# Four pieces of the next first layer ahead of a unit's pairs instead of three

## The chip, the cores and the metric

The kernel runs on one core of one Trainium2 chip. The metric is device time in microseconds (us) of one execution. Before the change three timed runs gave 1337.73, 1338.77 and 1339.29 us, a median of 1338.77 us.

## The reference, cut to what matters

The program is one layer of a diffusion backbone over 1024 latent tokens of width 1024. After a mixing half (convolution, Fourier mixing, attention, state space) comes the feed-forward half, which the change concerns:

```python
hx = modulate(rmsnorm(x_mid, g_norm_mlp[l]), sh2, sc2)
x = x_mid + gt2 * squared_relu_mlp(hx, w_ff1[l], b_ff1[l], w_ff2[l], b_ff2[l])

def squared_relu_mlp(h, w1, b1, w2, b2):
    return jnp.square(jax.nn.relu(h @ w1 + b1)) @ w2 + b2
```

The hidden width is 4096, everything is fp32 on the outside, and a final RMSNorm closes the program.

## The kernel before, in words

**Splitting.** A matmul operand is split into a high part (`w2h`, `fh`, `th`: a rounded copy made by ScalarE, ACT in the profile) and a low part (`w2l`, `fl`, `tl`: the difference). Three matmuls (high by high, high by low, low by high; `mm3w`, L1472) stand for one exact product. Weights are split by ACT (L1455) and GpSimd (POOL, L1456); hidden values by ACT (L1487) and VectorE (DVE, L1488).

**Units.** The hidden width is cut into 16 units of 256. A unit has a first layer (hidden values from `h`) and a second layer (their share of the output). Tokens stand in two halves of 512. From unit 2 on, the first layer of a unit is a recursion with seven products (`a11`, `a12`, `s1` to `s4`, `a22`) in place of eight. Each product is cut into two *pieces*, h0 and h1, of six matmuls each: 14 pieces, which `q_pieces` lists in that order. The weights of `s1` to `s4` are sums that DVE makes: L1605 (`s1`, into the one tile `ws`), L1607 (`s2`, in place), L1609 (`s3`, into a `w1r` tile), L1611 (`s4`, into `ws`).

**Pairs.** The second layer of a unit is four *pairs* p0 to p3. A pair is a recursion with seven products of three matmuls, in the order a0, a1, b1, b0, c0, c1, and d; the d of a pair is issued inside the next one, after its a1. They use PSUM banks: a0 in `fa`, a1 in `fc`, b1 in `fb`; b0 adds onto what a0 left in `fa`, c0 onto `fb`, c1 and then d onto `fa`. After each product DVE adds the bank, scaled, to the output tile `X` (`add_x`, L1493). So b0 may not start until DVE has read `fa` after a0, and d not until DVE has read it after c1.

**What runs beside.** While the pairs of unit u-1 run, pieces of the first layer of unit u are put between their products, so that DVE has time for its additions. In order, before the change: three pieces ahead (`a11` h0, h1 and `a12` h0); a0 of p0; one piece; a1, b1, b0; one piece; c0, c1; then p1, p2, p3 with one piece each between b0 and c0; one piece and the last d; and the remaining five pieces as a tail.

**What follows a piece.** After the second piece of a product come its `post` steps: L1624 copies a bank to `ft`, L1627 adds a bank to it (with `a12`: bank `qc`), L1479 and L1480 are the squared ReLU on ACT, and `part` (L1487, L1488) is the split. `s3` h0 triggers the split of hidden value (0,0). `a22` h1, the last piece of a unit, triggers a longer chain, over three entries: L1636 to L1638 (`sums`, from `s4` h1), the splits of t1, (1,0), t2, t3, t4, and L1645 (`sum_21`). These are what a0, a1, b1, b0, c1 and d of the next pairs read.

**What sets the order.** `Pieces.emit(AHEAD)` writes the instructions of PE, ACT, POOL and DVE in a fixed order. Before entry i of the sequence (a piece or one product) it issues the weight split of every entry up to i + 5 that has none yet. So where an entry stands also decides where its weight split stands in the queues of DVE (for `s1` to `s4`), ACT and POOL. Each engine works its queue in order. `w2h` and `w2l` have six buffers each. The DMAs on SP's queue are ordered by a scheduler.

Of the kernel before, what the change touches and what calls it, by code (L numbers as in the profile page):

```python
# [49 lines left out]
def body(tc, A, out, dbg=None):  # L50
# [1717 lines left out]
    with tc.manual_schedule(engines=MAN):  # L1768
        for u in range(2, NU2):
            q = q_pieces(u)  # L1770
            for _ in range(4 if u == 2 else 3):
                q.pop(0)()
            (plain_pieces if u == 2 else pair_pieces)(u - 1, q)
            for f in q:
                f()
        pc.emit(AHEAD)
# [158 lines left out]
```

## Time and profile before

| what | value |
|---|---|
| median of the timed runs | 1338.77 us |
| the profiled execution's own time | 1341.13 us |
| its span | 1339.0 us |
| granted TensorE clock, mean of the span | 0.947 |
| PE busy | 1197.4 us, 89% |
| DVE busy | 1068.4 us, 80% |
| POOL busy | 808.6 us, 60% |
| ACT busy | 652.7 us, 49% |

The span is the time from the first to the last instruction of one profiled execution. The loop that the change touches lies between about 721 and 1286 us of it. One turn of the loop takes 40.49 us (its wait stands at 814.14 us in one unit and at 854.63 us in the next). A row of a timeline gives the start, the duration, engine, line, operation, output<-inputs, and in brackets the engine's idle time just before and what ended it; "x2" means two instructions merged into the row. A row of the waits gives total us, times, longest us. A row by windows gives the window, its length, the busy us of PE, weight loads, DVE, ACT and POOL with the numbers of instructions, the granted clock, the DMA share and GB/s.

### The profile page before, as it was taken

How to read it: one execution, taken by the hardware profiler on the slowest of the kernel's cores; microseconds unless marked ns; L12 is line 12 of the kernel's file. 1: busy time of each engine (PE TensorE's matmuls, PEld its weight loads, DVE VectorE, ACT ScalarE, POOL GpSimd, SP SyncE). 2: the span in 40 equal slices, each digit the busy share in tenths (PEclk: the TensorE clock that was granted, in tenths of full speed). 3: DMA queues.
4: the chain of work that ended last, by engine and by line, in shares of the span. 5: the costliest groups of instructions: out<-in, count | busy, mean ns of one | idle time of the engine just before them, and what ended most of it. 6: DMA issues, size and time to landing. Idle time of an engine off the chain costs nothing.

```text
span 1339.0 us, 18718 instructions
## 1 busy us (share of the span) xinstructions
PE 1197.4 (89%) x6188; PEld 965.5 (72%) x6188; DVE 1068.4 (80%) x1636; ACT 652.7 (49%) x1337; POOL 808.6 (60%) x1002
## 2 busy tenths in 40 slices
PE   5889878898865999899999999999999999999996
PEld 3657656777655777777778777777877777777775
DVE  4775999869999768658695579888888888888867
ACT  5254333323446565554664445555545555444555
POOL 3825677372556734015367477777877778787754
PEclk9989898998975999898999999999999999999998
DMA  9455232161153544323121121111211112211113
GB/s 344 142 164 164 81 125 79 47 199 66 51 177 94 175 128 142 109 78 143 32 77 43 40 64 32 48 56 56 63 56 32 52 52 63 64 41 39 56 40 126
DMA packets 75058, 121.77 MB, mean 91 GB/s; under 512 B 16977, under 2 KB 35154, under 8 KB 74962
## 3 DMA queue, kind: packets, MB, share of 16 engines
q1 hardware_dynamic: 62802, 113.24, 26.9%
q10 hardware_dynamic: 12160, 7.34, 1.8%
q8 instruction: 49, 0.80, 0.3%
q14 instruction: 47, 0.39, 0.1%
HBM read 106.68 MB, written 13.88 MB: 90 GB/s over the span
## 4 chain that ended last, share of the span: by engine, by line
PE 48%; DVE 29%; ACT 5%; issue 4%; POOL 4%; DMA 3%; SPq 1%; ACTq 0%; DVEq 0%; POOLq 0%
PE fa L1472 11%; PE qa L1472 6%; PE qb L1472 5%; PE fb L1472 5%; DVE cacc L1015 5%; DVE tl L1488 3%; PE fc L1472 2%; DVE fl L1488 2%; PE f L1472 2%; PE p_t L1270 2%; PE mm L1097 2%; PE mm L1472 2%; DVE Ss L698 2%; DVE Ss L697 1%; DVE X L1493 1%
## 5 line engine op out<-in xcount | busy, mean ns | idle before, releaser
L1456 POOL TENSOR_TENSOR w2l<-w2r,w2h 128x128 fp32r<-128x128 f32 (+1 forms) x232 | 177.4, 766 | 75.3 <-ACT w2h L1455 68.1
L1493 DVE SCALAR_TENSOR_TENSOR X<-fa,gt2c,X 128x512 f32<-128x512 f32 x216 | 159.4, 745 | 13.0 <-PE fa L1472 13.0
L1455 ACT ACTIVATE w2h<-w2r 128x128 fp32r<-128x128 f32 (+1 forms) x232 | 85.8, 387 | 150.8 <-POOL w2r L1706 79.8
L1456 POOL TENSOR_TENSOR w2l<-w1r,w2h 128x256 fp32r<-128x256 f32 x136 | 108.5, 814 | 57.7 <-ACT w2h L1455 34.0
L235 POOL TENSOR_TENSOR wlo<-wraw,whi 128x1024 fp32r<-128x1024 f32 x30 | 75.2, 2508 | 102.0 <-ACT whi L233 82.9
L1493 DVE SCALAR_TENSOR_TENSOR X<-fb,gt2c,X 128x512 f32<-128x512 f32 x108 | 80.5, 745 | 35.4 <-PE fb L1472 35.3
L1456 POOL TENSOR_TENSOR w2l<-ws,w2h 128x256 fp32r<-128x256 f32 x84 | 67.9, 815 | 41.4 <-ACT w2h L1455 40.1
L1015 DVE SCALAR_TENSOR_TENSOR cacc<-cv,wdw,cacc 128x512 f32<-128x512 f32 x92 | 92.3, 1047 | 0.6
L364 PE MATMUL mm<-xl,whi 128*128 128x512 f32 x192 | 81.2, 424 | 3.8 <-DVE xl L220 3.8
L364 PE MATMUL mm<-xh,whi 128*128 128x512 f32 x192 | 77.3, 423 | 7.0 <-ACT xh L218 5.8
L1472 PE MATMUL fa<-th,w2h 128*128 128x512 f32 x156 | 63.2, 405 | 19.7 <-DVE X L1493 19.7
L364 PE MATMUL mm<-xh,wlo 128*128 128x512 f32 x192 | 80.6, 420 | 0.0
L1455 ACT ACTIVATE w2h<-w1r 128x256 fp32r<-128x256 f32 x136 | 53.9, 409 | 47.5 <-DVE w1r L1609 16.5
L1472 PE MATMUL qa<-cb,w2h 128*128 128x512 f32 x224 | 70.7, 397 | 0.7 <-ACT ft L1624 0.7
L1488 DVE TENSOR_TENSOR fl<-ft,fh 128x512 fp32r<-128x512 f32 x64 | 56.9, 906 | 12.8 <-ACT fh L1487 12.7
L1472 PE MATMUL fa<-th,w2l 128*128 128x512 f32 x156 | 61.7, 396 | 0.6 <-POOL w2l L1456 0.6
L1472 PE MATMUL fa<-tl,w2h 128*128 128x512 f32 x156 | 61.5, 394 | 0.0
L1013 POOL TENSOR_TENSOR pacc<-pacc,ptmp 128x512 f32<-128x512 f32 x24 | 37.4, 1559 | 29.8 <-ACT ptmp L1012 29.8
L1455 ACT ACTIVATE w2h<-ws 128x256 fp32r<-128x256 f32 x84 | 33.1, 410 | 42.4 <-DVE ws L1605 20.4
L1472 PEld LDWEIGHTS fa<-th,w2h 128*128 128x128 f32 x156 | 29.3, 188 | 30.8 <-DVE X L1493 25.2
L364 PEld LDWEIGHTS mm<-xh,whi 128*128 128x128 f32 x192 | 38.1, 201 | 18.4 <-ACT xh L218 7.2
L1472 PEld LDWEIGHTS qa<-cb,w2h 128*128 128x128 f32 x224 | 42.0, 188 | 11.2 <-ACT ft L1624 1.1
(788 smaller groups left out, 3945.3 us busy)
## 6 DMA issues: line engine op xcount, KB each, us to landing
w2r<-in_w_ff SPq DMA_DIRECT2D x68, 256.0 KB
wmB<-in_wmodB SPq DMA_DIRECT2D x32, 512.0 KB
w1r<-in_w_ff SPq DMA_DIRECT2D x64, 256.0 KB
wm<-in_wmodA SPq DMA_DIRECT2D x16, 512.0 KB
wraw<-in_w_in SPq DMA_DIRECT2D x12, 512.0 KB
x<-in_xT SPq DMA_DIRECT2D x8, 512.0 KB
wraw<-in_w_out SPq DMA_DIRECT2D x8, 512.0 KB
kr<-k_d SPq DMA_DIRECT2D x16, 256.0 KB
```

Source lines behind the costliest of these rows:

```text
L235: (lo_eng or G).tensor_tensor(lo, raw, hi.bitcast(F32), ALU.subtract)
L364: PE.matmul(o, a_[:, k, :], b_[hf][k], start=k == 0 and i == 0, stop=k == 7 and i == 2)
L698: V.tensor_tensor_scan(Ss[b_, i, g, ::-1], r_[b_], src[b_, g, ::-1], 0.0, ALU.mult, ALU.add)
L1013: G.tensor_tensor(pacc, pacc, t, ALU.add)
L1015: V.scalar_tensor_tensor(acc, x(k), w(k), acc, ALU.mult, ALU.add)
L1097: PE.matmul(o, a_[:, 2 * kk + c, :], b_, start=c == 0 and i == 0, stop=c == 1 and i == 2)
L1270: PE.matmul(po[:, j * 64:j * 64 + 64], ptt[:, i * P:(i + 1) * P], rv, start=i == 0, stop=i == 4, skip_group_check=True)
L1455: S.activation(hi, a, AF.Copy)
L1456: G.tensor_tensor(lo, a, hi.bitcast(F32), ALU.subtract)
L1472: PE.matmul(o, a_[:, i, :], m_, start=start and j == 0, stop=stop and j == 2, skip_group_check=True)
L1488: V.tensor_tensor(lo, t, hi.bitcast(F32), ALU.subtract)
L1493: return V.scalar_tensor_tensor(x, o, gt2(k), x, ALU.mult, ALU.add).ins
```

## The change

One number: for every unit four pieces are issued ahead of the pairs. For unit 2 it was four already.

```diff
         for u in range(2, NU2):
             q = q_pieces(u)
-            for _ in range(4 if u == 2 else 3):
+            for _ in range(4):
                 q.pop(0)()
             (plain_pieces if u == 2 else pair_pieces)(u - 1, q)
             for f in q:
```

The number of instructions stays as it was. In 13 turns (units 3 to 15) each piece from `a12` h1 on moves one place to the front: `a12` h1 stands ahead of a0 of p0, `s1` h0 after a0, `s1` h1 after b0, `s2` h0 and h1 in p1 and p2, `s3` h0 between b0 and c0 of p3, `s3` h1 before the last d, and four pieces are left for the tail.

**DVE at the start of a unit's pairs.** The splits of t1, (1,0) are `fl`, those of t2, t3, t4 are `tl`; X<-fa is the addition after a0. Before:

```order
L1638 TENSOR_TENSOR ft<-ft 128x512
L1488 TENSOR_TENSOR fl<-ft,fh 128x512 x2
L1488 TENSOR_TENSOR tl<-ft,th 128x512
L1645 TENSOR_TENSOR ft<-ft 128x512
L1488 TENSOR_TENSOR tl<-ft,th 128x512 x2
L1605 TENSOR_TENSOR ws<-w1r 128x512
L1493 SCALAR_TENSOR_TENSOR X<-fa,gt2c,X 128x512
L1627 TENSOR_TENSOR ft<-ft,qc 128x512
```

And now:

```order
L1638 TENSOR_TENSOR ft<-ft 128x512
L1488 TENSOR_TENSOR fl<-ft,fh 128x512
L1605 TENSOR_TENSOR ws<-w1r 128x512
L1488 TENSOR_TENSOR fl<-ft,fh 128x512
L1488 TENSOR_TENSOR tl<-ft,th 128x512
L1645 TENSOR_TENSOR ft<-ft 128x512
L1488 TENSOR_TENSOR tl<-ft,th 128x512 x2
L1627 TENSOR_TENSOR ft<-ft,qc 128x512
L1493 SCALAR_TENSOR_TENSOR X<-fa,gt2c,X 128x512
```

L1605, the weight sum of `s1`, has moved from the end of the splits to a place between the first two, and L1627 has moved ahead of the addition after a0.

**ACT at the same place.** w2h<-ws is the weight split of `s1` (h0, then h1), `fh` and `th` are the high parts of t1, (1,0), t2, t3, t4, and L1479 and L1480 the squared ReLU that follows L1627. Before:

```order
L1487 ACTIVATE fh<-ft 128x512 x2
L1487 ACTIVATE th<-ft 128x512
L1455 ACTIVATE w2h<-w2r 128x256
L1487 ACTIVATE th<-ft 128x512
L1624 COPY ft<-qa 128x512
L1487 ACTIVATE th<-ft 128x512
L1455 ACTIVATE w2h<-ws 128x256
L1455 ACTIVATE w2h<-w2r 128x256
L1479 ACTIVATE ft<-ft,colf 128x512
L1480 ACTIVATE ft<-ft 128x512
```

And now:

```order
L1487 ACTIVATE fh<-ft 128x512
L1455 ACTIVATE w2h<-ws 128x256
L1487 ACTIVATE fh<-ft 128x512
L1487 ACTIVATE th<-ft 128x512 x2
L1624 COPY ft<-qa 128x512
L1455 ACTIVATE w2h<-w2r 128x256
L1487 ACTIVATE th<-ft 128x512
L1479 ACTIVATE ft<-ft,colf 128x512
L1480 ACTIVATE ft<-ft 128x512
L1455 ACTIVATE w2h<-ws 128x256
```

The split of `s1` h0 now stands between the high parts of t1 and (1,0), and that of `s1` h1 behind the squared ReLU.

**DVE in the last pair, p3.** The X rows are the additions after b1 and b0, after c0 and c1, and after the last d; L1611 is the weight sum of `s4`, `fl` the low part of (0,0), and L1627 the addition of bank `qa` after `s3` h1. Before:

```order
L1493 SCALAR_TENSOR_TENSOR X<-fb,gt2c,X 128x512
L1493 SCALAR_TENSOR_TENSOR X<-fa,gt2c,X 128x512
L1611 TENSOR_TENSOR ws<-w1r,ws 128x512
L1493 SCALAR_TENSOR_TENSOR X<-fb,gt2c,X 128x512
L1493 SCALAR_TENSOR_TENSOR X<-fa,gt2c,X 128x512
L1488 TENSOR_TENSOR fl<-ft,fh 128x512
L1493 SCALAR_TENSOR_TENSOR X<-fa,gt2c,X 128x512
L1627 TENSOR_TENSOR ft<-ft,qa 128x512
```

And now:

```order
L1493 SCALAR_TENSOR_TENSOR X<-fb,gt2c,X 128x512
L1493 SCALAR_TENSOR_TENSOR X<-fa,gt2c,X 128x512
L1611 TENSOR_TENSOR ws<-w1r,ws 128x512
L1488 TENSOR_TENSOR fl<-ft,fh 128x512
L1493 SCALAR_TENSOR_TENSOR X<-fb,gt2c,X 128x512
L1493 SCALAR_TENSOR_TENSOR X<-fa,gt2c,X 128x512
L1627 TENSOR_TENSOR ft<-ft,qa 128x512
L1493 SCALAR_TENSOR_TENSOR X<-fa,gt2c,X 128x512
```

The low part of (0,0) has moved ahead of the additions after c0 and c1. On ACT its high part stands directly behind the split that waits for L1611.

## Rows read from the trace of the kernel before

**Rows 1.** By windows: one turn of the loop, busy times and clock.

```profile
804.99:845.48 40.49, 38.98 (x170) 31.42 (x168) 33.81 (x47) 21.26 (x49) 31.21 (x47) 1.00 0.16 52
```

**Rows 2.** Waits of PE from 720 to 1286 us.

```profile
PE fa L1472 <- DVE X L1493: 19.7, 13, 1.5
```

**Rows 3.** Timeline of PE, start of a unit's pairs.

```profile
804.99 0.39 PE L1472 MATMUL qa<-mh,w2h 128*128 128x512 f32 x1
...
814.14 0.50 PE L1472 MATMUL fa<-th,w2h 128*128 128x512 f32 x1 [1.51 <-DVE X L1493]
...
814.95 0.63 PE L1472 MATMUL qb<-c,w2h 128*128 128x512 f32 x2
...
816.35 0.40 PE L1472 MATMUL fb<-fh,w2h 128*128 128x512 f32 x1
...
817.75 0.40 PE L1472 MATMUL fa<-fh,w2h 128*128 128x512 f32 x1
```

**Rows 4.** Timeline of DVE, start of a unit's pairs.

```profile
807.25 1.81 DVE L1488 TENSOR_TENSOR fl<-ft,fh 128x512 fp32r<-128x512 f32 x2
808.99 1.22 DVE L1488 TENSOR_TENSOR tl<-ft,th 128x512 fp32r<-128x512 f32 x1
810.13 1.22 DVE L1645 TENSOR_TENSOR ft<-ft 128x512 f32<-128x512 f32 x1
...
812.75 0.68 DVE L1605 TENSOR_TENSOR ws<-w1r 128x512 f32<-128x512 f32 x1
813.35 0.74 DVE L1493 SCALAR_TENSOR_TENSOR X<-fa,gt2c,X 128x512 f32<-128x512 f32 x1
814.01 0.67 DVE L1627 TENSOR_TENSOR ft<-ft,qc 128x512 f32<-128x512 f32 x1
```

**Rows 5.** Timeline of ACT, start of a unit's pairs.

```profile
806.45 1.14 ACT L1487 ACTIVATE fh<-ft 128x512 fp32r<-128x512 f32 x2
...
813.46 0.42 ACT L1455 ACTIVATE w2h<-ws 128x256 fp32r<-128x256 f32 x1 [1.44 <-DVE ws L1605]
813.78 0.40 ACT L1455 ACTIVATE w2h<-w2r 128x256 fp32r<-128x256 f32 x1
814.72 0.73 ACT L1479 ACTIVATE ft<-ft,colf 128x512 f32<-128x512 f32 x1 [0.54 <-DVE ft L1627]
...
816.02 0.60 ACT L1455 ACTIVATE w2h<-w2r 128x256 fp32r<-128x256 f32 x2
```

**Rows 6.** Timeline of POOL, start of a unit's pairs.

```profile
808.47 1.18 POOL L1456 TENSOR_TENSOR w2l<-w1r,w2h 128x256 fp32r<-128x256 f32 x1
809.62 1.18 POOL L1456 TENSOR_TENSOR w2l<-w2r,w2h 128x256 fp32r<-128x256 f32 x1
810.76 0.91 POOL L1708 TENSOR_TENSOR w2r<-w2r 128x128 f32<-128x128 f32 x1
813.95 0.74 POOL L1456 TENSOR_TENSOR w2l<-ws,w2h 128x256 fp32r<-128x256 f32 x1 [2.28 <-ACT w2h L1455]
```

**Rows 7.** Timeline of PE, last pair of a unit.

```profile
792.53 0.40 PE L1472 MATMUL fa<-th,w2h 128*128 128x512 f32 x1
...
795.32 0.40 PE L1472 MATMUL fa<-th,w2h 128*128 128x512 f32 x1
...
797.42 0.39 PE L1472 MATMUL fa<-th,w2h 128*128 128x512 f32 x1
```

**Rows 8.** Timeline of DVE, last pair of a unit.

```profile
794.10 0.74 DVE L1493 SCALAR_TENSOR_TENSOR X<-fa,gt2c,X 128x512 f32<-128x512 f32 x1
794.76 0.68 DVE L1611 TENSOR_TENSOR ws<-w1r,ws 128x512 f32<-128x512 f32 x1
...
796.21 0.75 DVE L1493 SCALAR_TENSOR_TENSOR X<-fa,gt2c,X 128x512 f32<-128x512 f32 x1
797.06 0.69 DVE L1488 TENSOR_TENSOR fl<-ft,fh 128x512 fp32r<-128x512 f32 x1
```

**Rows 9.** Timeline of PE after the loop.

```profile
1295.92 1.12 PE L1472 MATMUL f<-fh,c 128*128 128x512 f32 x3 [2.33 <-ACT fh L1487]
```

## The prediction

> **What bounds the kernel now.** I read the busy times by windows first, then the waits of PE, then the timelines of the four engines around those waits. In one turn of the loop PE is busy for 38.98 of 40.49 us at a granted clock of 1.00, with DVE next at 33.81 us [rows 1]. So PE bounds the loop, and what it does not use is a single wait: 13 times about 1.5 us, 19.7 us in all, for an addition of DVE to X [rows 2]. The 1.51 us by which PE's 38.98 fall short of the turn's 40.49 are that one wait. So the most that any reordering can win here is 19.7 us, and every new gap of PE is paid in full, since nothing later in the turn gives time back.
>
> The place of the wait is b0 of the first pair. PE starts `a11` h0 of the next unit at 804.99; b0 should follow 33 matmuls later and starts at 814.14, after 1.51 us of idling [rows 3]. It waits for the addition after a0, which runs from 813.35 to 814.09 because DVE works through a packed chain of splits from 807.25 on, the weight sum L1605 last [rows 4]. The spacing of PE's matmuls without a wait is 1.40 us for six (814.95 to 816.35) [rows 3].
>
> **The change part by part.** No instruction is added or removed, so busy sums stay; only waits can move. I work in the clock of this turn and take everything up to the first `fl` at 807.25 as unmoved: the chain before it hangs on the tail, whose last four pieces are the same.
>
> *What goes.* One more piece stands ahead of b0, so PE reaches it 1.40 us later. If the addition were no later than now, 1.51 us would shrink to 0.11 us.
>
> *What comes first: the round trip in the splits.* L1605 now follows the first `fl`. The two `fl` take 1.81 us together, about 0.9 us each beside POOL's work [rows 4]. So L1605 starts at about 8.15 (I leave out the 800 from here) and, at the same rate, ends at about 9.1. ACT's split of `ws` waits for it (0.03 us from 813.43 to 813.46 now), the high part of (1,0) stands behind it and starts 0.32 us later (813.46 to 813.78), and takes 0.62 us (two in 1.14) [rows 5]. So that part ends at about 10.1 and the second `fl` starts at 10.15, where it now starts at about 8.15. Of these 2.0 us, 0.9 is L1605, which DVE had to do anyway; about 1.1 us is DVE idling.
>
> *Then the end of DVE's chain.* After it come five operations (`fl`, `tl`, L1645, `tl`, `tl`) and L1627. In the trace the five take from 8.15 to 12.75, 4.6 us, beside POOL's work; alone such an operation is followed after 0.60 us (812.75 to 813.35) [rows 4], so five take at least 3.0 us. POOL's part of this work has partly run during DVE's idle time, so I take a value between: 4.0 us, nearer to neither end. The five then end at 14.15 and L1627 at 14.8 (bounds: 13.85 and 15.4). Now L1627 ends at 14.68 [rows 4]. The addition after a0 follows it and ends about 0.7 later, at 15.5, in place of 14.09. b0, which PE reaches at 12.63 + 1.40 = 14.0, waits for 1.5 us, as it did: one addition more in the queue and the round trip have eaten the piece.
>
> On this stretch a rule of the Trainium skill can be weighed. POOL's weight splits take 1.18 us here against 0.74 us with DVE's own splits out of the way, and DVE's `tl` 1.22 us against 0.68 us for L1605 [rows 4, 6]. The page "SBUF — State Buffer", section "Who interferes with whom", says that a VectorE instruction with two SBUF inputs and a GpSimd one that reads SBUF share a port pair by an exclusive lock: the one that comes second waits for the whole of the first. By that the two would take turns, and a pair of them would need about 0.60 + 0.70 = 1.30 us (an estimate from the rows); the trace shows starts 1.14 us apart on DVE and 1.15 us on POOL [rows 4, 6], so it is close to the rule but not all of it. The rule speaks against this change, since POOL's split of `ws` now falls among the splits; it is among the rivals.
>
> *Then `s1` h1.* Its weight split is queued on ACT behind the squared ReLU, which waits for L1627. From the end of L1627 to ACT's next weight split pass 1.34 us (814.68 to 816.02) [rows 5], from the start of a split on ACT to the end of POOL's 1.23 us (813.46 to 814.69) [rows 5, 6]. So the low part is there 2.57 us after L1627, at about 17.4. PE needs it at the third matmul of `s1` h1, and four of six are left then, 0.94 us: c0 starts at about 18.35. Without waiting on this PE would start it at b0's 15.55 + 0.81 (b0 to the next piece) + 1.40 = 17.75. What stands before c0 is now the same set of 48 matmuls as what stands before a0 of the second pair in the trace, at 817.75 [rows 3]. So the first pair loses 0.6 us a turn. Bounds: L1627 at 13.85 gives c0 at 17.4, a gain of 0.35; at 15.4 a loss of 1.2.
>
> *The other place: the last d.* In p3 DVE must now do L1611 and the split of (0,0) between the additions after b0 and c1. Count from the start of b0. An addition starts 0.89 us after its product (795.32 to 796.21) and L1611 0.66 us after that addition (794.10 to 794.76) [rows 7, 8]: L1611 from 1.55 to 2.23. ACT's split of `ws` at 2.26, the high part of (0,0) from 2.58 to 3.20 by the steps above, the low part at 3.23. Then the addition after c0 at 3.83, 0.60 us on, and that after c1 at 4.5 to 5.25. PE reaches the last d after the same products as before in another order, 797.42 - 792.53 = 4.89 us after b0 [rows 7]. Now the addition ends at 796.96, 0.46 us ahead of d [rows 7, 8]; after the change it ends 0.36 us behind it. With the hand-over (0.05 us) I take 0.4 us a turn. POOL beside it could stretch L1611 and the split by 0.25 us each, as it does in the chain above (0.9 against 0.68), so up to 0.9 us; zero is the other bound, if the high part comes without the round trip.
>
> *At nothing:* the weight sums of `s2` and `s3` and their splits keep their distance of five entries to their use, under PE's products. The first uses of `ws` and of t1 and (1,0) on PE are ahead of b0, and by the steps above their splits end 0.2 us or more before PE comes, which is the thinnest of these covers; if it is gone, the first wait only moves to an earlier product. The DMAs of `w1r` and `w2r` are as many as before; the one that L1605 needs was issued a tail earlier. After the loop PE waits 2.33 us for a split [rows 9] in either order; I give that 1.5 us both ways, once.
>
> *The sum.* 0.6 + 0.4 = 1.0 us in each of 13 turns, 13 us. On the profiled execution's 1341.13 us that is 1354.1 us. The median of the timed runs is 1338.77 us, 2.36 us below that execution, so I predict 1351.8 us.
>
> **The rivals.**
>
> *The piece covers the wait: faster.* The place is b0. Had DVE and ACT no round trip, the addition after a0 would be one operation (0.60 us) later and PE 1.40 us later: 0.8 us less waiting in 13 turns, 10.4 us, 1328.4 us; with all of the wait gone 1319 us. For it: the wait is real and the piece longer than what it pays for. It decides if L1627 ends ahead of 14.2, since `s1` h1 is then no longer late. Against it: the order of the rows, in which L1605 stands between the splits on DVE and ACT both. Chance 0.12.
>
> *Nothing changes.* The round trip is hidden, the first pair wins up to 0.35 us and the last d loses 0.4 us: 1338 to 1340 us. For it: both numbers are within their bounds. Chance 0.10.
>
> *Only the last d costs.* The first pair comes out even and 13 times 0.4 us are left: 1344 us. Chance 0.15.
>
> *The lock.* If DVE and POOL take turns in full, three POOL operations (the `ws` split, the next weight split and L1708) fall among the five, each at about 0.7 us: 3.0 + 2.1 = 5.1 us in place of 4.0, so L1627 ends at 15.9, the first pair loses 1.7 us, and d 0.9 us: 34 us, 1373 us. (That is the rule of the page named above.) Against it: the measured 1.14 us of spacing. Chance 0.05.
>
> The forecast, both places paid for, has the remaining 0.58; alone it reaches from 1345 to 1361 us.
>
> **How the numbers follow.** The range 1338 to 1362 us leaves out the faster case (0.12) and the lock and other high ends (0.06). A change of 0.2%, 2.7 us, is about what a measurement of this kernel can tell from none. Slower by more than that: the forecast, the last d alone and the lock, 0.78; within it 0.10; faster 0.12.
>
> **What would show it.** In the profile after: PE's waits for X at `fa` should be two in each turn, b0 of p0 still at about 1.5 us and the last d at about 0.4 us, and a new wait of some 0.6 us of `qb` (`s1` h1) for `w2l` or `w2h`. DVE should show about 1 us of idling ahead of the second `fl`, ended by ACT, and ACT the split of `ws` waiting for L1605 there. A turn should take about 41.5 us in place of 40.49. The prediction is wrong if the wait at b0 falls under 1 us, if d does not wait, or if `s1` h1 finds its weights ready.

## The result: slower by 3.5%

The changed kernel takes 1383.64 us in the median of six runs (1376.32 to 1389.21), the kernel before 1338.11 us in six runs beside it. The ratio is 1.0346, 95% interval 1.0309 to 1.0383. I had forecast slower, but 1351.8 us with 1362 us as the upper end: the loss is 45.5 us and not 13.

The profiled execution (1389.21 us, span 1387.3 us) is the longest of the six. Its loop starts at 728.08 us, the other's at 721.63 us, although every engine has the same instructions in the same order up to there; so 6.4 us of the 48.2 us between the two spans are not the change's, and 41.8 us are left. The 12 turns from 770.22 to 1296.56 us take 526.34 us, where the same 12 turns took 488.99 us: 37.4 us. The rest of the program takes 4.4 us more. By windows of the changed kernel (columns as in [rows 1]): a turn, another turn, and two short stretches of the second:

```profile
944.89:987.69 42.80, 39.70 (x170) 31.26 (x168) 33.14 (x47) 20.80 (x49) 30.79 (x47) 1.00 0.15 50
856.20:900.55 44.35, 41.29 (x170) 32.37 (x168) 33.17 (x47) 20.48 (x49) 29.83 (x47) 0.96 0.15 48
869.20:872.60 3.40, 3.40 (x10) 2.62 (x9) 0.66 (x1) 1.00 (x2) 3.13 (x7) 0.50 0.00 0
873.00:876.40 3.40, 3.40 (x16) 2.72 (x16) 3.28 (x5) 1.23 (x4) 1.82 (x4) 1.00 0.24 80
```

There are two kinds of turn. One takes 42.80 us, 2.31 more than [rows 1]. The other takes 44.35 us, and in it TensorE runs a stretch at a granted clock of 0.50, that is 1.2 GHz in place of 2.4: 10 matmuls in 3.40 us against 16. Nine of the 13 turns have such a stretch, and it costs 1.55 us each. Eight of the nine lie in the 12 turns and make up 12.4 us of their 37.4 us. The other 25.0 us are 2.08 us a turn, less than 2.31: the turns of the kernel before run from 40.43 to 41.65 us, 40.75 us in the mean, and that of [rows 1] is one of the short ones.

The waits of PE from 720 to 1286 us; the row answers to [rows 2] (25 waits with the last unit's):

```profile
PE fa L1472 <- DVE X L1493: 33.8, 23, 1.7
```

**The first pair.** PE in a turn without the stretch (`a11` h0 starts at 944.89); the rows are b0, `s1` h1, its third and fourth matmul, and c0:

```profile
955.65 0.50 PE L1472 MATMUL fa<-th,w2h 128*128 128x512 f32 x1 [1.69 <-DVE X L1493]
...
956.71 0.73 PE L1472 MATMUL qb<-c,w2h 128*128 128x512 f32 x2
957.53 0.51 PE L1472 MATMUL qb<-c,w2l 128*128 128x512 f32 x1
957.88 0.63 PE L1472 MATMUL qb<-c,w2h 128*128 128x512 f32 x2
...
958.58 0.39 PE L1472 MATMUL fb<-fh,w2h 128*128 128x512 f32 x1
```

b0 waits for 1.69 us, no less than in [rows 3], and `s1` h1 takes 1.87 us in place of 1.40; it also starts 0.26 us later behind b0 (1.06 us in place of 0.81). c0 starts 13.69 us after `a11` h0; the same amount of work took 12.76 us (817.75 - 804.99) [rows 3]. The first pair loses 0.93 us. On DVE, in the turn from 856.20, with the rows that answer to [rows 4]:

```profile
858.73 0.95 DVE L1488 TENSOR_TENSOR fl<-ft,fh 128x512 fp32r<-128x512 f32 x1
859.60 0.95 DVE L1605 TENSOR_TENSOR ws<-w1r 128x512 f32<-128x512 f32 x1
861.61 0.81 DVE L1488 TENSOR_TENSOR fl<-ft,fh 128x512 fp32r<-128x512 f32 x1 [1.06 <-ACT fh L1487]
...
865.57 0.68 DVE L1627 TENSOR_TENSOR ft<-ft,qc 128x512 f32<-128x512 f32 x1
866.16 0.74 DVE L1493 SCALAR_TENSOR_TENSOR X<-fa,gt2c,X 128x512 f32<-128x512 f32 x1
```

DVE idles for 1.06 us until ACT has the high part of (1,0). ACT at that place, to set beside [rows 5]:

```profile
860.64 0.42 ACT L1455 ACTIVATE w2h<-ws 128x256 fp32r<-128x256 f32 x1 [2.37 <-DVE ws L1605]
860.97 0.62 ACT L1487 ACTIVATE fh<-ft 128x512 fp32r<-128x512 f32 x1
...
866.27 0.72 ACT L1479 ACTIVATE ft<-ft,colf 128x512 f32<-128x512 f32 x1 [1.98 <-DVE ft L1627]
867.03 0.63 ACT L1480 ACTIVATE ft<-ft 128x512 f32<-128x512 f32 x1
867.57 0.40 ACT L1455 ACTIVATE w2h<-ws 128x256 fp32r<-128x256 f32 x1
```

The split of `s1` h0 holds the high part behind it until L1605 is through, and the split of `s1` h1 starts 1.3 us after L1627 has released the squared ReLU.

**The last d.** PE's b0 of p3 and last d, then DVE between them, to set beside [rows 7, 8]:

```profile
888.08 0.40 PE L1472 MATMUL fa<-th,w2h 128*128 128x512 f32 x1
...
894.33 0.47 PE L1472 MATMUL fa<-th,w2h 128*128 128x512 f32 x1 [1.20 <-DVE X L1493]
```

```profile
889.63 0.74 DVE L1493 SCALAR_TENSOR_TENSOR X<-fa,gt2c,X 128x512 f32<-128x512 f32 x1
890.28 0.68 DVE L1611 TENSOR_TENSOR ws<-w1r,ws 128x512 f32<-128x512 f32 x1
892.05 0.81 DVE L1488 TENSOR_TENSOR fl<-ft,fh 128x512 fp32r<-128x512 f32 x1 [1.09 <-ACT fh L1487]
892.79 0.74 DVE L1493 SCALAR_TENSOR_TENSOR X<-fb,gt2c,X 128x512 f32<-128x512 f32 x1
893.45 0.73 DVE L1493 SCALAR_TENSOR_TENSOR X<-fa,gt2c,X 128x512 f32<-128x512 f32 x1
```

d starts 6.25 us after b0, where 4.89 us was free of waits [rows 7]: 1.36 us a turn. (PE's idle time of 1.20 us is counted from the modelled end of the matmul before.)

**The clock.** PE in the turn from 856.20, behind b0's wait of 1.68 us and the first matmuls of `s1` h1:

```profile
869.18 1.02 PE L1472 MATMUL qb<-c,w2h 128*128 128x512 f32 x2
870.00 0.63 PE L1472 MATMUL qb<-c,w2l 128*128 128x512 f32 x1
870.42 0.63 PE L1472 MATMUL fb<-fh,w2h 128*128 128x512 f32 x1
870.85 0.63 PE L1472 MATMUL fb<-fl,w2h 128*128 128x512 f32 x1
```

The matmuls stand 0.43 us apart in place of 0.23.

### The profile page after: what moved, and what is told of

Read it like the earlier page. It is cut to its first block, busy times and chain, and to the rows that moved or that the text cites. A ratio compares the mean times of both kernels' runs of the same rounds, so it can differ in the third digit from the quotient of the medians.

```text
span 1387.3 us, 18782 instructions
## 1 busy us (share of the span) xinstructions
PE 1218.8 (88%) x6188; PEld 974.7 (70%) x6188; DVE 1054.9 (76%) x1636; ACT 645.0 (46%) x1337; POOL 797.9 (58%) x1002
## 4 chain that ended last, share of the span: by engine, by line
PE 42%; DVE 20%; issue 12%; POOL 12%; DMA 4%; ACT 3%; SPq 0%; ACTq 0%; POOLq 0%; DVEq 0%
PE fa L1472 9%; POOL w2l L1456 6%; PE qa L1472 6%; PE fb L1472 5%; DVE cacc L1015 5%; PE fc L1472 2%; PE qb L1472 2%; PE p_t L1270 2%; PE mm L1472 2%; PE mm L1097 2%; DVE Ss L698 1%; DVE Ss L697 1%; PE f L1472 1%; PE p_t L1258 1%; DMA qq<-q_d 1%
## 5 line engine op out<-in xcount | busy, mean ns | idle before, releaser
L1456 POOL TENSOR_TENSOR w2l<-w2r,w2h 128x128 fp32r<-128x128 f32 (+1 forms) x232 | 164.8, 716 | 56.7 <-ACT w2h L1455 51.9
L1456 POOL TENSOR_TENSOR w2l<-w1r,w2h 128x256 fp32r<-128x256 f32 x136 | 105.3, 789 | 81.8 <-ACT w2h L1455 76.1
L1472 PE MATMUL fa<-th,w2h 128*128 128x512 f32 x156 | 66.3, 425 | 38.5 <-DVE X L1493 38.5
L1488 DVE TENSOR_TENSOR fl<-ft,fh 128x512 fp32r<-128x512 f32 x64 | 51.6, 807 | 37.2 <-ACT fh L1487 37.2
L1455 ACT ACTIVATE w2h<-w1r 128x256 fp32r<-128x256 f32 x136 | 51.1, 406 | 43.9 <-DVE w1r L1609 21.3
L1479 ACT ACTIVATE ft<-ft,colf 128x512 f32<-128x512 f32 x42 | 30.4, 723 | 67.6 <-DVE ft L1627 67.6
```

What stands on the lines that cost most here:

```text
L1455: S.activation(hi, a, AF.Copy)
L1456: G.tensor_tensor(lo, a, hi.bitcast(F32), ALU.subtract)
L1472: PE.matmul(o, a_[:, i, :], m_, start=start and j == 0, stop=stop and j == 2, skip_group_check=True)
L1479: S.activation(t, t if src is None else src, AF.Relu, bias=CF("b_ff1", f))
L1488: V.tensor_tensor(lo, t, hi.bitcast(F32), ALU.subtract)
```

## The experiments

Theory: the loss is three things: the round trip at the start of a unit's pairs with what it delays (0.93 us a turn), the split of (0,0) in p3 (1.36 us), and a clock that falls because of the first pair's waits. All kernels but the first and the last have four pieces ahead. The times are medians; the intervals are of the ratio to the kernel before, run beside them: it took 1339.81 us beside the first four experiments and 1341.95 us beside the last four, so kernels of different groups are better compared by their ratios. "Turn" is a usual one without the stretch at 1.2 GHz, "stretches" are those of the 13 turns. With three pieces ahead (first and last row) the place after the same 48 matmuls is a0 of the second pair and not c0.

| kernel | time us | ratio, 95% interval | turn us | c0 after `a11` h0, us | stretches |
|---|---|---|---|---|---|
| before | 1338.11 | 1 | 40.49 | 12.76 | 0 |
| changed | 1383.64 | 1.0309 to 1.0383 | 42.80 | 13.69 | 9 |
| split of (0,0) late | 1363.47 | 1.0162 to 1.0195 | 41.70 | 14.0 to 14.2 | 6 |
| sum of s1 early | 1358.13 | 1.0120 to 1.0167 | 41.81 | 12.62 | 0 |
| both | 1350.47 | 1.0063 to 1.0122 | 41.26 | 13.6 to 13.7 | 3 |
| split of s1 h1 early | 1363.02 | 1.0158 to 1.0200 | 42.17 | 12.97 | 0 |
| sum of s3 early | 1373.55 | 1.0226 to 1.0258 | 42.35 | - | 8 |
| split of (0,0) at b0 | 1357.89 | 1.0110 to 1.0144 | 41.57 | 13.69 | 4 |
| all mended | 1327.58 | 0.9883 to 0.9941 | 39.41 | 11.31 | 1 |
| before, sum of s1 early | 1336.78 | 0.9945 to 0.9988 | 39.96 | 12.27 | 0 |

### The split of (0,0) put back

```diff
-        pre_q7 = (lambda: part((0, 0), 11),)
+        pre_q7 = (lambda: None,) * 3 + (lambda: part((0, 0), 11),)
```

> Four pieces ahead as in the changed kernel, and only the split of (0,0) put back to where it stood before in DVE's order, behind the addition after c1 (three entries after s3 h0). Theory (the split, with its round trip over ACT, holds the addition after c1): the wait at the last d, 1.2 to 1.4 us a turn, goes to 0.1 us or less, a turn without a stretch at half clock falls from 42.80 to about 41.4 us, and the time from 1383.6 to about 1366 us. The waits of the first pair stay (1.7 us at b0), and if they alone draw the clock down, about 9 of 13 turns still have a stretch at half clock. Rival (DVE is simply behind in p3 since L1609 now stands ahead of the additions there): the wait at d falls only to about 0.7 us, the time to about 1375 us. Rival on the clock (it falls for a turn's idle time as a whole): the stretches vanish with d's wait and the time falls below 1355 us.

Measured: 1363.47 us. d does not wait any more, so the split did hold it. But the turn fell by 1.10 us and not by 1.36, since the wait at b0 grew from 1.7 to about 2.1 us; the kernel with both edits shows why. PE at b0, to set beside the 1.69 us above:

```profile
905.69 0.51 PE L1472 MATMUL fa<-th,w2h 128*128 128x512 f32 x1 [2.04 <-DVE X L1493]
```

Six stretches are left although d's wait is gone: the clock falls without that wait too.

### The sum of s1 early

```diff
-                if h == 0 and name == "s1":
+                if h == 1 and name == "a12":
                     st["ws"] = wf.tile([P, 4, P], F32, name="ws", tag="ws", bufs=1)
+                    ES.tensor_tensor(st["ws"], a21, a22, ALU.add)
                 ws = st.get("ws")
                 if h == 0:
-                    if name == "s1":
-                        ES.tensor_tensor(ws, a21, a22, ALU.add)
-                    elif name == "s2":
+                    if name == "s2":
```

> Four pieces ahead as in the changed kernel, and only the weight sum of s1 (L1605, here L1602) issued five places earlier on DVE, ahead of L1636, with the weight split left where it is. Theory (the round trip L1605, split of ws, high part of (1,0) delays DVE's chain, and with it the addition after a0 and the split of s1 h1): DVE's idling of about 1.06 us ahead of the second fl goes, the chain ends some 1.5 us sooner, the wait at b0 falls from 1.7 to under 0.4 us, c0 starts 12.2 to 12.6 us after a11 h0 in place of 13.7, the stretches at half clock vanish, the wait at d (1.2 us) stays, a turn takes about 41.4 us, the time is about 1350 us. Rival (the first pair is late since POOL's work beside DVE stretches the splits): the chain ends less than 0.8 us sooner and the wait at b0 stays over 1 us; time over 1365 us.

Measured: 1358.13 us. DVE's idling ahead of the second `fl` is gone, c0 comes at 12.62 us, and there is no stretch at 1.2 GHz. The chain ends 1.07 us sooner, and not 1.5 (L1627 ends 8.98 us after `a11` h0, 10.05 in the changed kernel): the five operations from the second `fl` to L1627 take about 4.9 us where they took 3.96 us. POOL's split of `ws` now runs among them (936.67 us, 1.18 us long) and not in DVE's idle time (861.14 us, 0.74 us), which is the likely reason. So the wait at b0 is still 0.6 to 0.8 us and the size was off:

```profile
899.92 0.51 PE L1472 MATMUL fa<-th,w2h 128*128 128x512 f32 x1 [0.62 <-DVE X L1493]
```

The round trip's place in the loss is shown.

### Both

> Four pieces ahead, the split of (0,0) late and the sum of s1 early, both as in the two kernels beside it. Theory: both waits go, no stretch at half clock is left in the loop, a turn takes about 40.0 us, and the time is about 1330 us, under the kernel before (1338 us). Rival (a piece more ahead costs by itself, as a fuller DVE queue): a turn stays over 40.5 us and the time at 1340 us or more.

Measured: 1350.47 us, 20 us over the expectation, and the rival's numbers. A turn takes 41.26 us: d does not wait, but the first pair is late by 0.9 us again. The late split of (0,0) delays the tail. Behind L1627 (from `qb`), the kernel with the early sum alone (first fence) starts L1636 2.15 us later, this kernel (second fence) 3.20 us later:

```profile
929.51 0.69 DVE L1627 TENSOR_TENSOR ft<-ft,qb 128x512 f32<-128x512 f32 x1 [2.02 <-PE qb L1472]
...
931.66 0.69 DVE L1636 TENSOR_TENSOR ft<-ft 128x512 f32<-128x512 f32 x1 [0.25 <-ACT ft L1480]
```

```profile
926.05 0.69 DVE L1627 TENSOR_TENSOR ft<-ft,qb 128x512 f32<-128x512 f32 x1 [1.00 <-PE qb L1472]
927.28 0.89 DVE L1488 TENSOR_TENSOR fl<-ft,fh 128x512 fp32r<-128x512 f32 x1 [0.55 <-ACT fh L1487]
...
929.25 1.22 DVE L1636 TENSOR_TENSOR ft<-ft 128x512 f32<-128x512 f32 x1
```

DVE now waits for ACT in the tail as well, and the whole chain of splits begins a microsecond later. It is not the piece more ahead that costs, as the rival had it, but where the split stands; the kernel with all places mended settles that.

### The split of s1 h1 early

```diff
-                while keys and at[keys[0]] <= i + ahead:
+                while keys and at[keys[0]] <= i + ahead + (keys[0][1:] == ("s1", 1)):
```

> Four pieces ahead as in the changed kernel, and only the weight split of s1 h1 issued one entry earlier, so that on ACT it stands ahead of the squared ReLU that waits for L1627. Theory: s1 h1 no longer waits for its weights (now about 0.26 us for the high and 0.46 us for the low part), c0 starts about 13.0 us after a11 h0 in place of 13.7, the wait at b0 stays at 1.7 us; 0.7 us a turn, 9 us, and time at about 1374 us if the stretches at half clock stay. If the clock falls because three waits stand close together here, some or all of the nine stretches go as well, down to 1360 us. Rival (the split of s1 h1 is late for POOL, not for ACT's queue): no change, 1383 us.

Measured: 1363.02 us. PE behind `a11` h0 at 893.98, b0, `s1` h1 and c0:

```profile
904.74 0.51 PE L1472 MATMUL fa<-th,w2h 128*128 128x512 f32 x1 [1.68 <-DVE X L1493]
...
905.55 0.63 PE L1472 MATMUL qb<-c,w2h 128*128 128x512 f32 x2
...
906.95 0.39 PE L1472 MATMUL fb<-fh,w2h 128*128 128x512 f32 x1
```

`s1` h1 takes 1.40 us again, 0.72 us a turn less up to c0 as expected, and the wait at b0 is the same. ACT's squared ReLU was what held it. And all nine stretches are gone, although b0 waits for 1.68 us and d still waits for 1.2 to 1.4 us in each turn. The early sum left the short waits of `s1` h1 and cut b0's, and there the clock did not fall either. So the place of the stretches is behind both together: of the ten kernels in the table, the five in which b0 waits for 1.3 us or more and `s1` h1 waits right behind it have three to nine stretches there, and the other five have none there. The gain is 0.72 times 13 and 1.55 times 9, 23 us, of which the medians show 20.6.

### The sum of s3 early

```diff
-                    elif name == "s3":
-                        ES.tensor_tensor(a21, a11, a21, ALU.subtract)
...
+                if h == 1 and name == "s2":
+                    ES.tensor_tensor(a21, a11, a21, ALU.subtract)
```

> Four pieces ahead as in the changed kernel, and only the weight sum of s3 (L1609) issued a pair earlier on DVE, with the split of s2 h1, so that it no longer stands ahead of the additions of p3. It measures how much of the wait at the last d (1.2 to 1.4 us a turn) comes from DVE being behind in p3. If the backlog is part of it (0.66 us: the addition after b0 starts 1.55 us after b0 in place of 0.89), the wait at d falls to about 0.7 us, the turn by 0.6 us, the time by 8 us to about 1375 us. If the round trip is all of it, nothing changes: 1383 us.

Measured: 1373.55 us. PE at d, to set beside the 1.20 us above:

```profile
933.71 0.47 PE L1472 MATMUL fa<-th,w2h 128*128 128x512 f32 x1 [0.64 <-DVE X L1493]
```

The step from the matmul ahead of d to d falls from 1.59 to 1.03 us, so 0.56 us of d's wait was DVE's backlog, and the rest (0.8 us) the split with its round trip.

### The split of (0,0) at b0

```diff
-    raw2 = {}
+    raw2, early = {}, {}
...
-        pre_q7 = (lambda: part((0, 0), 11),)
+        early[u] = lambda: part((0, 0), 11)
+        pre_q7 = (early[u],) if u == 2 else None
...
+                more = early[u + 1] if (p, name, i) == (3, "b", 0) else lambda: None
-                return lambda: pc.add((u, p, name), mm, (lambda: add_x(hf, k, bk[tag]),))
+                return lambda: pc.add((u, p, name), mm, (lambda: (add_x(hf, k, bk[tag]), more()),))
```

> Four pieces ahead as in the changed kernel, and only the split of (0,0) issued one entry earlier, with b0 of p3, so that it stands ahead of L1611 on DVE and ahead of the split that waits for L1611 on ACT. The low part still stands ahead of the additions after c0 and c1, but without a round trip. Theory (the round trip is what holds d): DVE's idling of 1.09 us goes, the wait at d falls to 0.3 us or less, without the tail coming later as it did when the split was put behind c1: the turn without a stretch at half clock falls by 1.1 to 1.3 us to about 41.6 us; time about 1367 us. Rival (any 0.6 us more of DVE work there holds d): the wait at d stays over 0.8 us, time over 1375 us.

Measured: 1357.89 us, a turn of 41.57 us. d starts 0.29 to 0.54 us after the matmul ahead of it, where it was 1.59 us or more and is 0.23 us without a wait. DVE in p3, to set beside the rows of the changed kernel above:

```profile
923.06 0.74 DVE L1493 SCALAR_TENSOR_TENSOR X<-fa,gt2c,X 128x512 f32<-128x512 f32 x1
923.72 0.68 DVE L1488 TENSOR_TENSOR fl<-ft,fh 128x512 fp32r<-128x512 f32 x1
924.32 0.68 DVE L1611 TENSOR_TENSOR ws<-w1r,ws 128x512 f32<-128x512 f32 x1
924.92 0.74 DVE L1493 SCALAR_TENSOR_TENSOR X<-fb,gt2c,X 128x512 f32<-128x512 f32 x1
925.58 0.74 DVE L1493 SCALAR_TENSOR_TENSOR X<-fa,gt2c,X 128x512 f32<-128x512 f32 x1
```

The same five operations take 3.26 us from the first to the end of the last where they took 4.55 us, with no idling. So the round trip, 1.09 us, is what holds d, and not the work of the split. The backlog that the early sum of `s3` took away is still there, so it costs only behind a round trip. The first pair waits as in the changed kernel (c0 at 13.69 us), yet the stretches are four and not nine; the five fewer are most of the 9 us by which the time came out under the expectation.

### All places mended

The edits of the early sum, the early split of `s1` h1 and the split at b0 together, and

```diff
-        post_q2 = (lambda: more(11, st["qc"]),)
+        post_q2 = (lambda: None, lambda: None, lambda: more(11, st["qc"]))
```

> Four pieces ahead with all places mended: the sum of s1 ahead of L1636, the split of s1 h1 an entry earlier, the split of (0,0) with b0 of p3, and L1627 after a12 put behind the addition after a0. Theory: the wait at b0 falls to about 0.2 us, s1 h1 and d do not wait, no stretch at half clock; a turn takes 39.2 to 39.8 us against 40.49 before, the time is 1322 to 1330 us, under both kernels. Rival (what is won at these places comes back as a later tail, as when the split of (0,0) alone was put off): a turn stays at 40.5 us or more, 1338 us or more.

Measured: 1327.58 us, 0.9912 of the kernel before (0.9883 to 0.9941), and 56 us under the changed kernel. One turn by windows:

```profile
888.09:927.50 39.41, 39.39 (x169) 31.24 (x168) 32.90 (x46) 20.96 (x49) 31.64 (x47) 1.00 0.19 54
```

PE is busy for 39.39 of 39.41 us. Nine turns of 12 take 39.4 to 39.8 us, two 40.3 and one 41.4 us; the one stretch at 1.2 GHz is in the last unit's turn, at another place. So four pieces ahead are not slow by themselves, once nothing that waits is put into the queues in front of the splits. That the fourth piece is what makes this kernel faster than the kernel before is not shown: three pieces with all these edits were not run, and three with the early sum alone are faster too.

### The kernel before with the early sum

```diff
-    raw2 = {}
+    raw2, nxt = {}, {}
...
-                    st["ws"] = wf.tile([P, 4, P], F32, name="ws", tag="ws", bufs=1)
+                    st["ws"] = nxt.get(u) or wf.tile([P, 4, P], F32, name="ws", tag="ws", bufs=1)
...
-                    if name == "s1":
+                    if name == "s1" and u == 2:
...
         def sums():
+            n = raws[u + 1]
+            nxt[u + 1] = wf.tile([P, 4, P], F32, name="ws", tag="ws", bufs=1)
+            ES.tensor_tensor(nxt[u + 1], n[2], n[3], ALU.add)
```

> The kernel before, three pieces ahead, with only the weight sum of s1 (L1605) issued ahead of L1636. In the kernel before it is the last operation of DVE's chain ahead of the addition after a0. Theory: that addition ends 0.3 to 0.6 us sooner, the wait at b0 falls from 1.51 to about 1.0 us, a turn to about 40.0 us, time about 1332 us, faster than before by about 0.4%. Rival (L1636 is pushed back by as much as the chain is shortened): no change, 1338 us.

Measured: 1336.78 us, 0.9967 of the kernel before (0.9945 to 0.9988). One turn by windows, to set beside [rows 1]:

```profile
887.32:927.28 39.96, 38.94 (x170) 31.45 (x168) 33.74 (x47) 21.14 (x49) 31.59 (x47) 1.00 0.17 54
```

The wait at b0 falls from 1.5 to 1.0 us, a turn to 39.96 us. So L1605 at the end of the chain was a third of the wait that the kernel before had there.

## Why the prediction was wrong

**Right: the direction and the places.** The round trip of L1605 was put at 1.1 us of idling and measured 1.06; b0's wait at 1.5 us, measured 1.69; both by the same releasers. That `s1` h1 waits behind the squared ReLU, and that d waits behind the split of (0,0), are shown by undoing each.

**The first pair, a little small.** I had c0 0.6 us late, it was 0.93. The step "everything up to the first `fl` at 807.25 as unmoved" was off by 0.27 us: that `fl` starts 2.53 us after `a11` h0 in place of 2.26, since POOL now has the split of `a12` h1 ahead of the pair's and meets DVE's sums (L1638 takes 1.11 us in place of 0.84). L1627's end, forecast at 14.8 on that clock, came at 15.04.

**The last d, mis-sized: 0.4 us forecast, 1.36 measured, above the bound of 0.9.** The step that failed is "an addition starts 0.89 us after its product". After b0 it starts 1.55 us later (888.08 to 889.63). L1609 stands ahead of p3's additions (at 886.19 us), they follow each other every 0.66 us while the products come every 0.69, and the backlog is carried to b0. The rows of the kernel before already said so: there the addition after b0 starts 1.57 us after b0 (792.53 to 794.10) [rows 7, 8], also with L1609 ahead:

```profile
792.84 0.68 DVE L1609 TENSOR_TENSOR w1r<-w1r 128x512 f32<-128x512 f32 x1
```

I took the 0.89 us from c1 (795.32 to 796.21), where the backlog has been worked off. So the lag of another product was taken, and the move of L1609 has changed nothing there. That is 0.66 us; the kernel with the sum of `s3` early gave 0.56 of it back. The low part beside POOL (0.74 us to the next start in place of 0.60) and two longer hand-overs (0.09 and 0.10 us) are the rest.

**The clock, left out: 14 us.** The sum had no term for it. I took the granted clock of 1.00 in the loop [rows 1] as given, and 1.5 us of waiting a turn had left it there. The changed kernel puts some 0.7 us of short waits right behind b0's, and in nine turns TensorE runs at 1.2 GHz for a while. Taking only those short waits away took the stretches away. With d at 1.36 us, the first pair at 0.93 and nine stretches the same sum gives 44 us, where the medians differ by 45.5 us. Some of this closeness is luck, as the turn of [rows 1] is a short one: against the mean turn, 2.08 us in each of 13, the sum is 41 us, close to the 41.8 us that the two profiled executions leave to the change.

**The rivals.** The piece does not cover the wait, as the order of the rows said. That the round trip was what stood against it is shown by the early sum, which takes c0 from 13.69 to 12.62 us, and by the mended kernel, in which b0 follows the matmul ahead of it after 0.42 us in ten turns of 13, where it was 2.08 us. The lock between DVE and POOL in full would have ended L1627 at 15.9; it came at 15.04, between the forecast and the lock. Of its three POOL operations only two ran wholly among DVE's five (863.49 and 864.18 us); by the same sum these two make 4.4 us, and the five took 3.96. In the kernel with the early sum all three run among them, and the five take 4.9 us where the sum makes 5.1. So the full lock fits neither, but in the second case it is close.

**Open.** Why nine turns and not thirteen: the waits in turns with and without a stretch are alike up to it (b0 at 10.76 us after `a11` h0 in both). With the same first pair there were nine, eight and four stretches in three kernels whose turns differ in length. They do not seem to come at random: with the split of (0,0) at b0 every third turn has one (those from 806.36, 932.72, 1058.94 and 1185.18 us), with both edits every fifth, and the changed kernel has seven in a row at its end. What this regularity hangs on no run separated, so the number of stretches could not have been forecast from the waits alone.

## What to carry to other kernels

When work is issued earlier in engines that keep their order, follow every wait that goes with it into every queue: an operation that costs 0.7 us cost twice that here because a split on another engine that waits for it stood in front of the chain's own. An engine that keeps pace with its supplier by a few hundredths of a microsecond carries a backlog on, so an operation put ahead of such a run is paid at its end; take the lag between a product and its addition from the row of that product, and not from another's. And when a change leaves new short waits behind a long one on TensorE, put the price of a slower clock into the range.

## What the runs showed of the hardware

- The granted clock fell to 0.50 with no wait of TensorE over 1.7 us in the turn, and matmuls of 512 columns then stood 0.43 us apart in place of 0.23; a stretch cost 1.55 us.
- A wait of 1.68 us in each turn with another of 1.2 to 1.4 us later left the clock at 1.00 in all 13 turns; with about 0.7 us of short waits behind the first it fell in 9 of 13, and in 8 and 4 of 13 in two kernels with the same first pair. With the short waits but 0.6 to 0.8 us at first it did not fall.
- Two executions with the same instructions up to the loop reached it 6.4 us apart (721.63 and 728.08 us).
